# Two attention changes in one kernel: stationary values with a transposed output, and score banks shared with the transposes

## The chip, the cores and the metric

The kernel runs on one core of a Trainium2 chip. The metric is the device time of one execution in microseconds (us). TensorE is PE (its weight loads are PEld), VectorE is DVE, ScalarE is ACT, GpSimd is POOL, and SyncE (SP) issues the DMAs.

## The reference, cut to what matters

A two-layer decoder trunk on 256 tokens with model width 1024. Layer A has differential attention (6 head pairs of 2 x 64), layer B plain causal attention (12 heads of 64; with one block of 256 keys the block selection selects nothing more). Each layer also attends with 4 heads to a memory of 256 rows, and has a squared-ReLU MLP of width 4096.

```python
# memory attention, both layers: 4 heads of 64, 256 keys
p = softmax(einsum('bshd,bmhd->bhsm', qm, mk) * 64 ** -0.5);  o = einsum('bhsm,bmhd->bshd', p, mv)
# layer B: the same with a causal mask, 12 heads of 64
# layer A: w = softmax(s0) - lam * softmax(s1);  o = rmsnorm(w @ v)
x = x + concat([o_self, o_mem]) @ w_out
x = x + relu(rmsnorm(x) @ w_up) ** 2 @ w_down
```

All is float32 at the borders.

## The kernel before, in words

Every projection splits its weights and its activations into a rounded part and a rest (`wh`/`wl` for weights, `h`/`l` for activations) and sums three products. `chunk` (L308) loads one of 192 weight chunks of 128 x 1024, ACT casts it to `wh` (L328), DVE subtracts to `wl` (L330). In a mixer `nat_block` (L475) projects all 256 tokens on 512 columns, `rope` (L493 to L510) or `evac_to` (L485) takes the result out of the two `acc` banks, attention follows, and `out_proj` (L737) accumulates pair by pair in four `acc` banks. The MLPs are L785 and L787 (`wide`) and, for the last product, L846.

Attention works on two heads at a time (a "pair"; m0 and m1 are the two memory pairs, 0 to 5 the others). The steps of a pair:

- `scores` (L514): four transposes of q and k into a `t` bank (L525), a copy, the score matmuls (L555) with the 64 rows of head 0 in the upper half of the array and those of head 1 in the lower half. In layer A a causal pair first adds the mask by PE (L548); in layer B DVE adds it (`hide`, L562). Both heads lie in one buffer `s` of two PSUM banks, of which there is one. One DVE reduction for both heads (L565), the scaling of the maxima (L567, L569), then four ACT exponentials (L573); they accumulate the row sums only in layer A's causal pairs.
- `plain_T` (L614), for the memory pairs of both layers and for layer B's six pairs, so ten in all: three or four transposes of each head's probabilities (L593) into a `t` bank, then a copy (L626 or L627).
- `plain_out` (L632): the transposed probabilities are the stationary operand and the values the moving one. A 65th column of ones in the values gives the row sum. Per pair 6 (causal) or 8 (memory) matmuls with 65 columns (L644); then DVE takes a reciprocal (L652) and multiplies (L653) into `o`.
- `finish_o` (L598): two transposes of `o` (L603) into another `t` bank, then the split into `h` (ACT, L608) and `l` (DVE, L609).
- Layer A's six pairs go through `diff_T` and `diff_out` instead (transposes also L593, values L691 to L693), and then through `finish_o` with a gain.

PSUM has 8 banks: four `acc`, two `t`, and the one two-bank buffer `s`.

The order of the instructions on every engine is set when the program is built. `Plan` collects the steps with an assumed duration each, and a list scheduler sends each engine the ready step with the lowest number; a table `EARLY` shifts the numbers by kind of step and layer. A step also needs its buffers free: `acc`, `w`, `wh`, `wl` are taken first come first served. On the chip each engine then works in that order and waits on semaphores.

Of the kernel before, what the change touches and what calls it, by code (L numbers as in the profile page):

```python
# [29 lines left out]
KINDS = ("w", "mem", "nat", "stat", "rope", "score", "pt", "pv", "fin", "evac", "prep")  # L30
# [191 lines left out]
def tile_hybrid(ctx: ExitStack, tc: tile.TileContext, xt, memt, wall, gains, fgain, subln, lam, trig, out):  # L222
# [6 lines left out]
    caps = {"w": 4, "wh": 6, "wl": 6, "acc": 4, "s": 1, "t": 2, "u": 2, "sq": 2, "sqa": 2, "dg": 2,  # L229
# [38 lines left out]
    mv = fixed([128, 2, 4, 65], "mv")  # L268
    vb = fixed([128, 2, 12, 65], "vb")
# [4 lines left out]
    wu = psum.tile([128, 2, 512], F32, name="wu", tag="s0", bufs=1)  # L274
    for _ in range(34):
        nc.tensor.matmul(wu[:, 0, 0:128], ones_b, ones_b, start=True, stop=True)
# [12 lines left out]
    for t in (mv, vb):  # L289
        nc.gpsimd.memset(t[:, :, :, 64:65], 1.0)  # L290

# [222 lines left out]
    def scores(srcs, skeys, causal, sums):  # L514
# [11 lines left out]
        P.add(("pe", 4 * 85, turn), skeys, [ps])  # L526
# [10 lines left out]
        nm = fixed([128, 2, ns], "nm")  # L537
# [3 lines left out]
        sp = buf("s", [128, 2, 512], F32, psum)  # L541
# [3 lines left out]
        def qkmm():  # L545
            for hd in range(2 * pm):
                for i in range(2):
                    nc.tensor.matmul(sp.t[:, hd, i * 256:i * 256 + 128], ident_b, mask_b, start=i == 0, stop=False,  # L548
                                     skip_group_check=True)
            for qb in range(2):  # L550
                c = slice(0, n0) if qb == 0 else slice(n0, n0 + 256)
                for i, (a, b) in enumerate(passes):
                    for hd in range(2):
                        r = slice(hd * 64, hd * 64 + 64)
                        nc.tensor.matmul(sp.t[:, hd, c], qk[a].t[r, qb * 128:(qb + 1) * 128],  # L555
# [4 lines left out]
        def hide():  # L560
            o = sp.t[:, :, 0:512].rearrange("p h (b n) -> p h b n", b=4)[:, :, 0:3:2]
            nc.vector.tensor_tensor(o, o, mask_b[:, None, None, :].to_broadcast([128, 2, 2, 128]), op=OP.add)  # L562

        def mxx():
            nc.vector.tensor_reduce(nm, sp.t[:, :, 0:width].rearrange("p h (s n) -> p h s n", s=ns), axis=AX.X,  # L565
                                    op=OP.max)
            nc.vector.tensor_scalar_mul(nm, nm, -0.125)  # L567
            if causal:
                nc.vector.tensor_tensor(nm[:, :, 1], nm[:, :, 1], nm[:, :, 2], op=OP.min)  # L569

        def ex(hd, qb):
            c = slice(0, n0) if qb == 0 else slice(n0, n0 + 256)
            nc.scalar.activation(p[hd].t[:, c], sp.t[:, hd, c], AF.Exp, scale=0.125, bias=nm[:, hd, qb:qb + 1],  # L573
                                 **({"accum_out": ss[:, hd, qb:qb + 1]} if sums else {}))
        cols = 2 * 384 if causal else 2 * 512
        P.add(("pe", (4 if whole else 3) * (cols / 2.4 + 50) + 240 * pm, qkmm), qk, [sp])
        if causal and not pm:
            P.add(("dve", t_dve(512), hide), [sp], [sp])
        P.add(("dve", t_dve(2 * width) + 400, mxx), [sp], [("nm", id(nm))])
        for qb in range(2):  # L580
            for hd in range(2):
                n = n0 if qb == 0 else 256
                P.add(("act", 144 + 93 * sums + 0.835 * n, lambda hd=hd, qb=qb: ex(hd, qb)),
                      [sp, ("nm", id(nm))], [(p[hd], qb), ("ss", id(ss), 2 * hd + qb)])
        if sums:
            P.add(("dve", 90, lambda: nc.vector.reciprocal(rs, ss)), [("ss", id(ss), i) for i in range(4)],
# [583 lines left out]
```

## Time and profile before

| | us |
|---|---|
| median of 3 runs | 623.08 (623.02 to 623.41) |
| the profiled execution: its own time | 624.98 |
| its span (first to last instruction) | 623.2 |
| PE busy | 606.8 (97%) |
| DVE, ACT, POOL busy | 447.0, 373.3, 68.2 |

The median is 1.90 below the time of the profiled execution. By time in the profile: the start to 13 us, layer A's mixer to 137 us, layer A's MLP to 315 us, layer B's mixer to 437 us, layer B's MLP and the last norm to the end.

How to read it: an engine's busy time is the union of its instructions. Matmuls overlap, so the cost of a matmul in a row of them is the distance from its start to the next start, not its own length. A float32 matmul shows as two records, a transpose and an fp32r matmul as one.

### The profile page before, as it was taken

Reading aid. Unit: us, or ns where it says so; the run is one execution under the profiler, and the core shown is the slowest. Engines: PE = TensorE matmul, PEld = TensorE weight load, DVE = VectorE, ACT = ScalarE, POOL = GpSimd, SP = SyncE. Lnnn points to the kernel's source line nnn. Section 1 sums busy time; section 2 is a strip of 40 time slices with the busy share of each in tenths; the row PEclk is TensorE's granted clock in tenths of the full one; section 3 lists DMA queues with packets and bytes.
Section 4 is the critical chain, followed back from the end, with each engine's and each line's share of the span. In section 5 each row is a group of like instructions: output and inputs, shape, how many; then the busy total and the mean of one; then the engine's idle time right before and its main releaser. Section 6 shows DMA issues by size and latency. Waiting matters only on the chain.

```text
span 623.2 us, 9883 instructions
## 1 busy us (share of the span) xinstructions
PE 606.8 (97%) x3706; PEld 529.5 (85%) x3706; DVE 447.0 (72%) x764; ACT 373.3 (60%) x712; POOL 68.2 (11%) x80
## 2 busy tenths in 40 slices
PE   7988999999999999999999999999999999999995
PEld 5766778998888888888889989999888888888874
DVE  5998886778978866556785676786998788544434
ACT  6856876867766754444764655555776766433422
POOL 1532011212000000101000111310300000000002
PEclk8998999999999999999999999999999999999998
DMA  7835442345756555555566243433456556656601
GB/s 250 309 135 169 141 163 103 111 153 151 252 183 199 178 197 201 181 191 192 181 225 211 83 158 107 164 136 121 151 194 208 179 196 193 193 192 197 200 7 68
DMA packets 30865, 106.32 MB, mean 171 GB/s; under 512 B 3681, under 2 KB 4193, under 8 KB 30817
## 3 DMA queue, kind: packets, MB, share of 16 engines
q1 hardware_dynamic: 30816, 105.69, 51.7%
q8 instruction: 29, 0.48, 0.3%
q14 instruction: 20, 0.16, 0.1%
HBM read 104.62 MB, written 1.05 MB: 170 GB/s over the span
## 4 chain that ended last, share of the span: by engine, by line
PE 90%; DVE 3%; ACT 3%; DMA 2%; issue 1%; SPq 1%; POOL 0%; ACTq 0%; DVEq 0%; POOLq 0%
PE acc L785 29%; PE acc L475 17%; PE acc L787 14%; PE acc L737 7%; PE s L846 7%; PE t L846 7%; PE t L644 2%; PE s L555 2%; PE t L593 1%; DVE wl L330 1%; DMA xT<-xt 1%; PE t L525 1%; DMA w<-wall 1%; ACT B L573 1%; ACT wh L328 1%
## 5 line engine op out<-in xcount | busy, mean ns | idle before, releaser
L330 DVE TENSOR_TENSOR wl<-w,wh 128x512 fp32r<-128x512 f32 (+1 forms) x256 | 246.0, 978 | 92.0 <-ACT wh L328 88.7
L328 ACT CAST wh<-w 128x512 fp32r<-128x512 f32 (+1 forms) x256 | 208.2, 837 | 132.1 <-PE t L846 41.5
L785 PE MATMUL acc<-xn,wh 128*128 128x512 f32 x512 | 178.8, 395 | 0.0
L787 PE MATMUL acc<-xn,wl 128*128 128x256 f32 x512 | 142.4, 278 | 0.0
L785 PEld LDWEIGHTS acc<-xn,wh 128*128 128x128 f32 x512 | 96.2, 188 | 22.1
L475 PE MATMUL acc<-wh,xn 128*128 128x512 f32 (+1 forms) x320 | 96.1, 368 | 3.0 <-ACT xn L344 2.9
L787 PEld LDWEIGHTS acc<-xn,wl 128*128 128x128 f32 x512 | 96.3, 188 | 0.0
L785 PE MATMUL acc<-B,wh 128*128 128x512 f32 x256 | 88.8, 394 | 0.0
L787 PE MATMUL acc<-B,wl 128*128 128x256 f32 x256 | 71.1, 278 | 0.0
L475 PEld LDWEIGHTS acc<-wh,xn 128*128 128x128 f32 x320 | 58.2, 194 | 13.3 <-ACT xn L344 3.5
L785 PEld LDWEIGHTS acc<-B,wh 128*128 128x128 f32 x256 | 48.0, 188 | 11.2
L475 PE MATMUL acc<-wl,xn 128*128 128x512 f32 (+1 forms) x160 | 57.2, 358 | 0.0
L428 POOL TENSOR_TENSOR sqa<-sqa,sq 128x256 f32<-128x256 f32 x35 | 30.3, 866 | 231.3 <-ACT sq L427 230.0
L737 PE MATMUL acc<-B,wh 128*128 128x256 f32 x256 | 51.6, 290 | 0.0
L787 PEld LDWEIGHTS acc<-B,wl 128*128 128x128 f32 x256 | 48.1, 188 | 0.0
L758 ACT COPY u<-acc 128x256 f32<-128x256 f32 x64 | 23.5, 370 | 37.9 <-PE acc L787 37.6
L737 PEld LDWEIGHTS acc<-B,wh 128*128 128x128 f32 x256 | 41.6, 191 | 0.0
L846 PE MATMUL s<-wh,B 128*128 128x512 f32 x128 | 39.6, 391 | 0.8 <-DVE qh L878 0.8
L502 POOL TENSOR_TENSOR ropet<-ropes,trig 128x256 f32<-128x256 f32 x24 | 26.3, 1113 | 126.5 <-ACT ropes L493 92.0
L846 PE MATMUL t<-wh,B 128*128 128x512 f32 (+1 forms) x128 | 37.9, 379 | 0.0
L737 PE MATMUL acc<-B,wl 128*128 128x256 f32 x128 | 36.2, 283 | 0.0
L760 DVE TENSOR_TENSOR u<-u,acc 128x256 f32<-128x256 f32 x64 | 26.4, 417 | 12.8 <-ACT u L758 12.7
(183 smaller groups left out, 848.3 us busy)
## 6 DMA issues: line engine op xcount, KB each, us to landing
w<-wall SPq DMA_DIRECT2D x188, 512.0 KB, 4.2
w<-wall SPq DMA_DIRECT2D x8, 256.0 KB, 7.1
B<-memt SPq DMA_DIRECT2D x2, 512.0 KB, 7.2
w<-memt SPq DMA_DIRECT2D x2, 512.0 KB, 3.7
xT<-xt SPq DMA_DIRECT2D x1, 512.0 KB, 8.1
out<-qh SPq DMA_DIRECT2D x2, 256.0 KB, 2.8
out<-ql SPq DMA_DIRECT2D x2, 256.0 KB, 2.2
xT<-xt SPq DMA_DIRECT2D x2, 128.0 KB, 3.3
```

Source lines behind the costliest of these rows:

```text
L328: P.add(("act", t_act(n), lambda sl=sl: nc.scalar.copy(h.t[:, sl], w.t[:, sl])), [(w, x) for x in q], [(h, x) for x in q])
L330: P.add(("dve", t_dve(n), lambda sl=sl: nc.vector.tensor_sub(l.t[:, sl], w.t[:, sl], h.t[:, sl].bitcast(F32))), [(w, x) for x in q] + [(h, ...
L428: P.add(("pool", t_pool(S), lambda: nc.gpsimd.tensor_tensor(self.acc.t, self.acc.t, sq.t, op=OP.add)), [sq, self.acc], [self.acc])
L475: nc.tensor.matmul(pss[hf].t[:, c0:c1], a(k)[:, ts], b.t[:, o + c0:o + c1], start=(k == 0 and i == 0), stop=(k == KT - 1 and i == 2))
L502: nc.gpsimd.tensor_tensor(t.t[:, :, o:o + 32], zs.t[:, :, 32 - o:64 - o], b(sin[:, o:o + 32]), op=OP.mult)
L555: nc.tensor.matmul(sp.t[:, hd, c], qk[a].t[r, qb * 128:(qb + 1) * 128], qk[b].t[r, S:S + c.stop - c.start], start=(qb == 0 and i == 0 and ...
L737: nc.tensor.matmul(o, a.t[:, ws], x(k), start=(n == 0 and m % 2 == 0 and i == 0), stop=(n == KT - 1 and i == 2), skip_group_check=True)
L758: P.add(("act", t_act(S, True), lambda u=u, mi=mi, ps=ps: nc.scalar.copy(u.t[:, mi], ps.t[:, S:])), [ps], [(u, mi)])
L760: P.add(("dve", t_dve(S), lambda u=u, mi=mi, ps=ps: nc.vector.tensor_add(u.t[:, mi], u.t[:, mi], ps.t[:, :S])), [ps, (u, mi)], [(u, mi)])
L785: nc.tensor.matmul(ps.t, wh.t[:, ws], x_.rearrange("p a s -> p (a s)"), start=start, stop=stop, skip_group_check=True)
L787: nc.tensor.matmul(ps.t[:, 0:S], wl.t[:, ws], x_[:, 0], start=False, stop=stop, skip_group_check=True)
L846: nc.tensor.matmul(ps.t[:, c0:c1], a, b.t[:, c * 512 + c0:c * 512 + c1], start=(k == k0 and i == 0), stop=(k == 31 and i == 2), skip_group ...
```

## The change

- `plain_out`: the values (128 keys x 64 columns) become the stationary operand and the transposed probabilities the moving one, 256 columns at a time (128 for the second key block of a causal pair). Head 0 writes partitions 0 to 63 of the bank and head 1 partitions 64 to 127, so the output is already transposed. The column of ones, the reciprocal and the multiplication go; so does `finish_o` for these ten pairs. ACT and DVE split straight from the bank (L649, L650 of the changed kernel).
- `plain_T`: the probabilities are scaled by the reciprocal row sum before they are turned, by a new step `norm`: four per pair, each on DVE or on ACT as the scheduler finds (L620, L621). The row sums now come from the exponentials in all pairs.
- `scores`: the two-bank buffer `s` goes; each head gets a bank of the class `t`, which now has four. The mask of layer B, the maxima and their scaling run once per head.
- `mlp_last` takes its four banks from `t`.
- The assumed durations of several PE steps and the whole table `EARLY` are replaced, so that the order on every engine changes from start to end.

```diff
-EARLY.update(wA=70, wB=-117, memA=52, memB=-51, natA=8, natB=-63, statA=100, statB=11, ropeA=-76, ropeB=80, scoreA=89,
-             scoreB=-39, ptA=71, ptB=19, pvA=-30, pvB=158, finA=163, finB=-9, evacA=41, evacB=129, prepA=63, prepB=90)
+EARLY.update(wA=40, wB=60, memA=148, memB=-117, natA=82, natB=-5, statA=-94, statB=-135, ropeA=-84, ropeB=120,
+             scoreA=-74, scoreB=-42, ptA=95, ptB=19, pvA=-40, pvB=163, finA=201, finB=-81, evacA=-113, evacB=66,
+             prepA=25, prepB=98, normA=95, normB=-89)
...
-    caps = {"w": 4, "wh": 6, "wl": 6, "acc": 4, "s": 1, "t": 2, "u": 2, "sq": 2, "sqa": 2, "dg": 2,
+    caps = {"w": 4, "wh": 6, "wl": 6, "acc": 4, "t": 4, "u": 2, "sq": 2, "sqa": 2, "dg": 2,
...
-        sp = buf("s", [128, 2, 512], F32, psum)
+        sp = [bank("t") for _ in range(2)]
...
-        def mxx():
-            nc.vector.tensor_reduce(nm, sp.t[:, :, 0:width].rearrange("p h (s n) -> p h s n", s=ns), axis=AX.X,
-                                    op=OP.max)
-            nc.vector.tensor_scalar_mul(nm, nm, -0.125)
+        def mxx(hd):
+            m = nm[hd]
+            nc.vector.tensor_reduce(m, sp[hd].t[:, 0:width].rearrange("p (s n) -> p s n", s=ns), axis=AX.X, op=OP.max)
+            nc.vector.tensor_scalar_mul(m, m, -0.125)
...
+        cut = 128 if causal else 256
+        @early("norm")
+        def norm(hd, qb):
+            c = slice(0, cut) if qb == 0 else slice(cut, cut + 256)
+            m = c.stop - c.start
+            x, r = p[hd], (lambda: rs[:, hd, qb:qb + 1])
+            P.add([("dve", 130 + 0.52 * m, lambda: nc.vector.tensor_scalar_mul(x.t[:, c], x.t[:, c], r())),
+                   ("act", t_act(m, False, True), lambda: nc.scalar.activation(x.t[:, c], x.t[:, c], AF.Copy, scale=r()))],
+                  [(x, qb), ("rs", id(rs))], [(x, qb)], port=True)
...
         def pv():
-            first = True
-            for qb in range(2):
+            for kb in range(2):
+                q0 = 128 if causal and kb else 0
                 for hd in range(2):
-                    c = (2 * qb + hd) * 65
-                    for j, kb in blocks[qb]:
-                        nc.tensor.matmul(ps.t[:, c:c + 65], pp[hd].t[:, j * 128:(j + 1) * 128], v(kb, hd), start=first,
-                                         stop=(j, kb) == blocks[qb][-1], skip_group_check=True)
...
+                    nc.tensor.matmul(ps.t[hd * 64:hd * 64 + 64, q0:S], v(kb, hd), pp[hd].t[:, kb * S:kb * S + S - q0],
+                                     start=kb == 0, stop=kb == 1, skip_group_check=True)
...
-        def scale():
-            c = ps.t[:, 0:260].rearrange("p (a e) -> p a e", a=4)
-            nc.vector.reciprocal(ri, c[:, :, 64])
-            nc.vector.tensor_tensor(o.t.rearrange("p a (b e) -> p (a b) e", b=2), c[:, :, 0:64],
-                                    ri[:, :, None].to_broadcast([128, 4, 64]), op=OP.mult)
-        P.add(("dve", t_dve(S) + 200, scale), [ps], [o])
-        finish_o(o, kt, T)
+        P.add(("act", t_act(S, True), lambda: nc.scalar.copy(T.h(kt), ps.t[:, 0:S])), [ps], [T.hk(kt)])
+        P.add(("dve", t_dve(S), lambda: nc.vector.tensor_sub(T.l(kt), ps.t[:, 0:S], T.h(kt).bitcast(F32))),
+              [ps, T.hk(kt)], [T.lk(kt)])
```

Three places in the order. **The first** is PE in layer B's mixer, at the values of the memory pair m0 (`t<-mv` is that product, `acc` a projection, `B` a ring buffer of attention). Before:

```order
L475 MATMUL acc_3636<-wh_3525,xn_67 128x256
L644 MATMUL t_3775<-mv_78,B_685_3753 128x65 x8
L475 MATMUL acc_3642<-wh_3525,xn_67 128x256
...
L555 MATMUL s_3795<-qh_3773 128x256 x2
...
L603 MATMUL t_3813<-ident_123,o_3793 128x128 x2
```

With the change:

```order
L589 MATMUL t_3786<-ident_123,B_692_3748 128x128 x4
L473 MATMUL acc_3666<-wh_3544,xn_67 128x256
L473 MATMUL acc_3666<-wl_3565,xn_67 128x256
...
L589 MATMUL t_3798<-ident_123,B_692_3748 128x128 x4
...
L646 MATMUL t_3820<-B_696_3796,mv_78 64x256 x4
L473 MATMUL acc_3666<-wh_3605,xn_67 128x256
```

Eight matmuls of 65 columns and the two transposes of `o` became four of 256 columns on 64 output rows, and the turns of the two heads now stand apart.

**The second** is PE at layer A's first two causal pairs (4 and 5), at the mask and score matmuls. Before, with both pairs in the one buffer `s`:

```order
L548 MATMUL s_660<-mask_b_127,ident_b_125 128x128
L555 MATMUL s_660<-qh_650 128x128 x2
L555 MATMUL s_660<-qh_650 128x256 x2
L475 MATMUL acc_682<-wh_600,xn_67 128x512
...
L548 MATMUL s_732<-mask_b_127,ident_b_125 128x128
L555 MATMUL s_732<-qh_657 128x128 x2
L555 MATMUL s_732<-qh_657 128x256 x2
```

With the change:

```order
L553 MATMUL t_633<-qh_625 128x128
L553 MATMUL t_636<-qh_625 128x128
L553 MATMUL t_633<-qh_625 128x256
L553 MATMUL t_636<-qh_625 128x256
L523 MATMUL t_650<-ident_123,B_180_544 128x128 x4
...
L553 MATMUL t_675<-qh_665 128x128
L553 MATMUL t_678<-qh_665 128x128
L553 MATMUL t_675<-qh_665 128x256
L553 MATMUL t_678<-qh_665 128x256
```

The second pair has banks of its own (`t_675`, `t_678`) and stands 6 projection matmuls behind the first, where 24 stood before.

**The third** is DVE late in layer A's mixer, from the maxima of m1 to its scaling. Before:

```order
L565 TENSOR_REDUCE nm_155<-s_1026 128x4
L567 TENSOR_SCALAR nm_155<-nm_155 128x4
L330 TENSOR_TENSOR wl_1083<-w_943,wh_1069 128x512 x2
L652 RECIPROCAL ri_160<-t_1072 128x4
L653 TENSOR_TENSOR o_1097<-t_1072,ri_160 128x256
```

With the change:

```order
L564 TENSOR_REDUCE nm_158<-t_1172 128x2
L565 TENSOR_SCALAR nm_158<-nm_158 128x2
L629 COPY ppx_73<-t_1197 128x512
L564 TENSOR_REDUCE nm_159<-t_1174 128x2
L565 TENSOR_SCALAR nm_159<-nm_159 128x2
L328 TENSOR_TENSOR wl_1230<-w_1054,wh_1085 128x512 x2
L328 TENSOR_TENSOR wl_1242<-w_1120,wh_1182 128x512
L582 RECIPROCAL rs_161<-ss_160 128x4
L328 TENSOR_TENSOR wl_1242<-w_1120,wh_1182 128x512
L620 TENSOR_SCALAR B_205_673<-B_205_673,rs_161 128x256 x2
```

Before, the turn of m1 needed only the maxima and the exponentials; now the reciprocal, a weight split that stands ahead of it and the scaling come between. On PE, 24 matmuls of `out_proj`, the turns and values of m0 and the scores of pair 2 stand between the scores of m1 and its first turn.

Elsewhere in layer A, PE's first matmul for the norm's statistics (L436, L434 of the changed kernel) stands behind 87 projection matmuls instead of 45, with 9 more before the memory block's instead of 51.

## Rows read from the trace of the kernel before

**Rows 1.** The page: busy time of the engines.

```profile
PE 606.8 (97%) x3706; PEld 529.5 (85%) x3706; DVE 447.0 (72%) x764; ACT 373.3 (60%) x712; POOL 68.2 (11%) x80
```

**Rows 2.** Busy time by stage (stretch, its length, PE, PEld, DVE, ACT, POOL, then granted PE clock, DMA share, GB/s): layer A's mixer in its first two parts, layer A's MLP, layer B's mixer, layer B's MLP up to its last matmuls.

```profile
13.00:55.00 42.00, 40.00 (x181) 30.70 (x180) 39.00 (x77) 28.96 (x64) 17.07 (x18) 0.99 0.65 223
55.00:100.00 45.00, 42.62 (x253) 33.61 (x252) 36.94 (x85) 32.68 (x94) 6.44 (x8) 0.96 0.42 140
...
137.00:315.00 178.00, 178.00 (x1028) 155.57 (x1027) 133.12 (x188) 107.72 (x170) 10.89 (x11) 1.00 0.59 190
315.00:437.00 122.00, 122.00 (x977) 115.51 (x976) 85.72 (x161) 70.21 (x145) 15.02 (x14) 1.00 0.46 151
437.00:602.00 165.00, 165.00 (x861) 141.16 (x859) 112.53 (x146) 93.83 (x137) 5.17 (x7) 1.00 0.55 179
```

**Rows 3.** Waits of the whole run, those of PE in layer A's mixer and ACT's for weights: what waited, for what, us in total, times, longest us.

```profile
PE s L548 <- ACT B L573: 1.7, 1, 1.7
PE acc L475 <- ACT ropes L493: 1.5, 2, 0.9
...
PE t L603 <- DVE o L653: 0.7, 1, 0.7
...
ACT wh L328 <- DMA w<-wall: 5.4, 5, 3.4
```

**Rows 4.** PE in order of time in layer A (start, length, line, operation, tiles; in brackets the idle time before and what ended it): the wait for the buffer `s`, and two of the projection matmuls behind it.

```profile
57.21 0.38 PE L548 MATMUL s<-mask_b,ident_b 128*128 128x128 bf16 x4 [1.68 <-ACT B L573]
...
59.40 1.06 PE L475 MATMUL acc<-wh,xn 128*128 128x512 f32 x2
60.25 0.63 PE L475 MATMUL acc<-wl,xn 128*128 128x512 f32 x1
```

**Rows 5.** The granted clock just behind that wait (columns as in rows 2).

```profile
58.30:61.70 3.40, 3.40 (x10) 2.65 (x9) 3.26 (x8) 1.50 (x3) 0.93 (x2) 0.52 0.45 154
```

**Rows 6.** PE in order of time in layer B: the values of a memory pair, of a causal pair, and the transposes of an `o`, each with the projection matmuls around it.

```profile
347.24 0.28 PE L475 MATMUL acc<-wh,xn 128*128 128x256 f32 x1
347.35 1.89 PE L644 MATMUL t<-mv,B 128*128 128x65 f32 x16
349.06 0.36 PE L475 MATMUL acc<-wh,xn 128*128 128x256 f32 x1
349.26 0.28 PE L475 MATMUL acc<-wl,xn 128*128 128x256 f32 x1
...
361.85 0.38 PE L603 MATMUL t<-ident,o 128*128 128x128 f32 x2
361.99 0.48 PE L475 MATMUL acc<-wh,xn 128*128 128x512 f32 x1
362.30 0.39 PE L475 MATMUL acc<-wl,xn 128*128 128x512 f32 x1
362.53 0.39 PE L475 MATMUL acc<-wh,xn 128*128 128x512 f32 x1
...
380.35 1.45 PE L644 MATMUL t<-vb,B 128*128 128x65 f32 x12
381.61 0.37 PE L475 MATMUL acc<-wh,xn 128*128 128x256 f32 x1
```

**Rows 7.** PE in order of time in layer A: float32 score matmuls of a causal pair, the three values matmuls of a layer A pair (L691 to L693, two records each, the first shown) and the next projection, and the score matmuls of a memory pair.

```profile
48.92 0.93 PE L555 MATMUL s<-qh 64*128 64x128 f32 x8
49.78 0.51 PE L475 MATMUL acc<-wh,xn 128*128 128x512 f32 x1
...
76.68 0.38 PE L691 MATMUL t<-B,B 128*128 128x128 f32 x2
...
77.26 0.48 PE L475 MATMUL acc<-wh,xn 128*128 128x512 f32 x1
...
77.81 0.40 PE L475 MATMUL acc<-wh,xn 128*128 128x512 f32 x1
78.14 1.14 PE L555 MATMUL s<-qh 64*128 64x256 f32 x8
79.20 0.55 PE L593 MATMUL t<-ident,B 128*128 128x128 f32 x3
```

**Rows 8.** Groups of instructions by line and shape (count, busy us, mean ns of one, idle before): weight splits, maxima, accumulator reads, the scaling into `o`, the split of the output, the reciprocal, a small DVE scaling.

```profile
L330 DVE TENSOR_TENSOR wl<-w,wh 128x512 fp32r<-128x512 f32 x128 | 88.2, 723 | 16.5 <-ACT wh L328 15.6
...
L565 DVE TENSOR_REDUCE nm<-s 128x6 f32<-128x768 f32 x12 | 11.4, 951 | 0.1
L573 ACT ACTIVATION_READ_ACCUMULATOR B<-s,nm 128x1 f32 x24 | 4.9, 206 | 0.0
L653 DVE TENSOR_TENSOR o<-t,ri 128x256 f32<-128x256 f32 x10 | 4.3, 425 | 0.6
L609 DVE TENSOR_TENSOR B<-t,B 128x256 fp32r<-128x256 f32 x10 | 4.2, 420 | 3.3 <-ACT B L608 3.3
L608 ACT CAST B<-t 128x256 fp32r<-128x256 f32 x10 | 3.7, 371 | 3.4 <-PE t L603 3.1
L652 DVE RECIPROCAL ri<-t 128x4 f32<-128x4 f32 x10 | 1.8, 178 | 6.3 <-PE t L644 6.2
L453 DVE TENSOR_SCALAR dg<-ident,rstd 128x128 f32<-128x128 f32 x4 | 1.0, 282 | 0.0
```

More of the change, by code (lines that the diff above doesn't have):

```diff
@@ L513, in scores @@
     @early("score")
-    def scores(srcs, skeys, causal, sums):
+    def scores(srcs, skeys, causal):
         ps = bank("t")
@@ L525, in turn @@
                 nc.tensor.transpose(ps.t[:, i * 128:(i + 1) * 128], s(), ident)
-        P.add(("pe", 4 * 85, turn), skeys, [ps])
+        P.add(("pe", 4 * 110 + 85, turn), skeys, [ps])
         if whole:
@@ L536, in scores @@
         ns = 3 if causal else 2
-        nm = fixed([128, 2, ns], "nm")
+        nm = [fixed([128, ns], "nm") for _ in range(2)]
         ss, rs = [fixed([128, 2, 2], n) for n in ("ss", "rs")]
@@ L585, in scores @@
-        if sums:
-            P.add(("dve", 90, lambda: nc.vector.reciprocal(rs, ss)), [("ss", id(ss), i) for i in range(4)],
-                  [("rs", id(rs))])
+            nc.scalar.activation(p[hd].t[:, c], sp[hd].t[:, c], AF.Exp, scale=0.125, bias=nm[hd][:, qb:qb + 1],
+                                 accum_out=ss[:, hd, qb:qb + 1])
+        P.add(("pe", (1 if whole else 0.75) * width * 4 / 2.4 + 300 + 240 * pm, qkmm), qk, sp)
+        for hd in range(2):
+            if causal and not pm:
+                P.add(("dve", t_dve(S), lambda hd=hd: hide(hd)), [sp[hd]], [sp[hd]])
+            P.add(("dve", t_dve(width) + (420 if causal else 210), lambda hd=hd: mxx(hd)), [sp[hd]], [("nm", id(nm[hd]))])
+            for qb in range(2):
+                n = n0 if qb == 0 else 256
+                P.add(("act", 237 + 0.835 * n, lambda hd=hd, qb=qb: ex(hd, qb)),
+                      [sp[hd], ("nm", id(nm[hd]))], [(p[hd], qb), ("ss", id(ss), 2 * hd + qb)])
@@ L588, in scores @@
+        P.add(("dve", 90, lambda: nc.vector.reciprocal(rs, ss)), [("ss", id(ss), i) for i in range(4)],
+              [("rs", id(rs))])
         return p, rs
@@ L603, in turn, with plain_T @@
                 nc.tensor.transpose(ps.t[:, qb * 128:(qb + 1) * 128], o.t[:, qb], ident)
-        P.add(("pe", 170, turn), [o], [ps])
-        if gain is not None:
-            split_scaled(lambda: ps.t[:, 0:S], [ps], gain, T, kt, True)
-            return
-        P.add(("act", t_act(S, True), lambda: nc.scalar.copy(T.h(kt), ps.t[:, 0:S])), [ps], [T.hk(kt)])
-        P.add(("dve", t_dve(S), lambda: nc.vector.tensor_sub(T.l(kt), ps.t[:, 0:S], T.h(kt).bitcast(F32))),
-              [ps, T.hk(kt)], [T.lk(kt)])
-    @early("pt")
-    def plain_T(p, causal):
+        P.add(("pe", 305, turn), [o], [ps])
+        split_scaled(lambda: ps.t[:, 0:S], [ps], gain, T, kt, True)
+    def plain_T(p, rs, causal):
         n = 3 if causal else 4
```

92 lines of the change are left out of this document (35 added, 57 removed).

## The prediction

> **What bounds the kernel now.** I read the page first: PE is busy 97% of the span [rows 1]. The table by stage says where the rest is: PE is idle 2.0 us between 13 and 55 us and 2.4 us between 55 and 100 us, that is, in layer A's mixer alone; in layer A's MLP, in layer B's mixer and in layer B's MLP it is busy for all of 178, 122 and 165 us [rows 2]. DVE has 39 of 42 us taken in layer A's first part, but 86 of 122 in layer B's mixer [rows 2]. So a microsecond that PE needs less in layer B's mixer should come off the time, and in layer A's mixer it does so only where PE is not waiting. The waits are few: PE waited once for the score buffer `s` (1.7), twice for an `acc` bank that the rope still held (1.5 together), once for an `o` (0.7) [rows 3]. Behind the wait for `s` the granted clock was 0.52 for 3.4 us, the lower of its two levels, after PE had stood idle 1.68 us [rows 4, 5]; two projection matmuls took 0.85 us there, 0.43 each [rows 4], where they start 0.23 apart at the full clock [rows 6].
>
> **The sum, part by part.** It is made against the profiled execution (624.98, span 623.2) and taken from the median of 623.08, which is 1.90 lower.
>
> *Transposes of `o` gone.* The two transposes hold PE for 0.14 us, and the second projection behind them starts 0.31 later instead of 0.23, so 0.22 in all [rows 6]. Ten pairs lose them: 2.2 us. PE is the bound there, so all of it counts.
>
> *Values as the stationary operand.* Before, a memory pair holds PE for 1.71 us and a causal pair for 1.26, and either delays what follows by another 0.08 (0.20 from start to start instead of 0.12) [rows 6]: 1.79 and 1.34. The new form, two heads in two column halves, is not in this trace. The nearest rows are layer A's float32 scores, with the same columns and the two heads in two row halves. Eight records of 256 columns take 1.06 us there, four of 128 with four of 256 take 0.86 [rows 7]. The start is 0.33 behind the last projection instead of 0.23, so 0.10 is lost ahead [rows 7], and I leave 0.08 behind. The new prices are 1.24 and 1.04, and the gain is 4 x 0.55 + 6 x 0.30 = 4.0 us.
> The bounds come from the price of one record. A float32 record of 128 columns on the whole array takes 0.097 us (six in 0.58) [rows 7], one of 256 some 0.19. If the halves ran one after the other, a memory pair would cost 8 x 0.19 + 0.18 = 1.7 and a causal pair 4 x 0.29 + 0.18 = 1.3, a gain of 0.2 us over the ten. If they overlapped wholly and nothing were lost at the ends, 0.8 and 0.6: a gain of 8.6. I take 4.0, since the row halves are the same trade and carry these losses.
> A rule of the Trainium skill speaks against it. The row first: on layer B's projections each matmul has a weight load of its own (977 and 976 [rows 2]), all on the same rows of the array, and they start 0.12 apart, so the load hides behind the matmul before it [rows 6]. The Trainium skill ("TensorE: Matmul & The Clock Gate", Part 3) says that a weight load overlaps matmuls in flight only when the row groups differ, which two column halves don't offer. By that rule this term would be 0.2 us and not 4.0; the trace agrees with it for the row halves and not for the full-width loads just named.
>
> *Work put on DVE and ACT.* Ten pairs get four scalings each. DVE's nearest rows are 0.28 for 128 columns and 0.43 for a product of 256 [rows 8], so 11 to 17 us over both engines; 0.18 + 0.43 per pair goes, 6 us [rows 8]. Forty exponentials now also read the accumulator, 0.21 each, 8 us on ACT [rows 8]. The maxima run once per head, with 0.5 us more per pair. In layer B, where 34 us of DVE and 52 of ACT are free under PE [rows 2], I cost this at nothing; if that cover went, it would cost what the third rival says. In layer A only two pairs are scaled. POOL's work and the DMAs stay what they were, and the issue order of the first DMAs is unchanged; POOL sums the memory's squares later.
>
> *Waits that go.* With a bank per head, the scores of pair 5 need no exponentials of pair 4 to be done. That takes away the 1.7 and eight matmuls at 0.20 too much each, 1.6 [rows 4, 5]. The wait for `o` (0.7) [rows 3] has no `o` left to wait for. Sum: 4.0.
>
> *Waits that come.* The statistics matmul of layer A now stands 42 projections later and has 9 ahead of the memory block instead of 51, so that the memory block waits longer for the first rope: between 0 and two more of the longest such wait; I take one, 0.9 [rows 3]. In layer A's last part the path from a pair's scores to its turn now runs through a reciprocal and scalings. For m1 DVE does two maxima (0.5 + 0.17 each), a copy and three weight splits (0.72 each [rows 8]), a reciprocal and two scalings: some 5.3 us. PE has 24 matmuls of `out_proj` at 0.12, eight transposes, the values of m0 and the scores of pair 2: 2.9 + 0.9 + 1.2 + 1.2 = 6.2 us (0.12 from [rows 6], the others from above and [rows 7]). It fits with 0.9 to spare; I put in one wait of the size of the longest, 1.7 [rows 3], as an allowance over the four pairs there, between 0 and four of them. At layer B's end 12 projections (1.4 us [rows 6]) cover the last split (0.37 and 0.42 [rows 8] and the hand-overs): 0 to 0.8, I take 0.4. Sum: 3.0.
>
> The total is -2.2 - 4.0 - 4.0 + 3.0 = **-7.2 us**: 617.8 for a profiled execution, **615.9** for the median. A measurement of this kernel can tell 0.2% from no change, 1.25 us.
>
> **The rivals.**
>
> *The halves run one after the other.* For it: no row shows column halves at work. Against it: full-width weight loads hide [rows 6], and the row halves overlap [rows 7]. The values then give 0.2: -3.4 us, 619.7. The rule of the Trainium skill named above would make it so.
>
> *The wait for `s` was a wait for weights.* ACT's casts waited 5.4 us for weights, 3.4 at the longest [rows 3], and the exponentials that PE waited for stood behind such a cast. If the weights are as late now, PE waits for the cast instead and the 3.3 us of the wait and its slow stretch stay: -3.9 us, 619.2. For it: that DMA's cause, the release of weight buffers by a DVE with 39 of 42 us taken [rows 2], isn't touched.
>
> *Layer A's last part waits for the scalings* (the slower one). At m0, m1 and pairs 2 and 3 the turns stand close behind their scores on PE, on a DVE that does the weight splits of `out_proj` in between. It decides once the path of a pair grows by more than the 0.9 to spare, one weight split and a hand-over. Then each of the four places waits 1.7, and the clock falls behind three of them, 1.6 each: 11.6 instead of my 1.7, so -7.2 + 9.9 = +2.7 us, 625.8. Against it: between 55 and 100 us DVE has 8 of 45 us free and ACT 12 [rows 2], and the scalings are short.
>
> *Layer A's waits all go.* PE's idle 4.4 us and the slow stretch (1.6) vanish [rows 2, 5] and nothing comes back: -2.2 - 4.0 - 6.0 = -12.2 us, 610.9.
>
> **How the numbers follow.** My forecast gets 0.45; weights as late as before 0.22; halves one after the other 0.14; all waits gone 0.10; scalings late 0.09. The range is 611.5 to 622.0: it takes in the forecast with both ends of its waits, the two weaker gains, and most of the case in which all waits go; it leaves out the slower case, the tails of the weaker gains above 622 and the best part of the last one. Faster by over 0.2% (below 621.8) hold the forecast, the best case and most of the two weaker gains: 0.81. Within 0.2% lie weaker gains that meet more waits than I allow: 0.08. Slower gets the rest: 0.11.
>
> **What would show it.** In layer B's mixer PE should still be busy throughout, and the stage should be shorter by 8 x 0.22 + 2 x 0.55 + 6 x 0.30 = 4.7 us. A memory pair's values should hold PE for about 1.06 us and a causal pair's for 0.86 (1.5 and 1.2 if the halves take turns). PE's wait for exponentials and the stretch at half clock near 58 us should be gone; if ACT's weight cast is awaited there instead, the second rival holds. Waits of PE's transposes for DVE or ACT between 85 and 110 us would be the third. The MLPs should keep their lengths. A layer B stage that shrinks by less than 3 us, or any wait of PE in it over 1 us, would make the prediction wrong at its core.

## The result and the profile after

The changed kernel takes **618.41 us** (four runs, 617.45 to 618.53) against 623.25 for the kernel before (four runs, 623.02 to 623.68). The ratio is 0.9918, with an interval of 0.9901 to 0.9935: 4.8 us less, where 7.2 were forecast. The direction was right and the time is inside the range. The profiled execution is the one of 617.45, span 615.7.

The page first: PE has 76 matmul records less than in [rows 1], as the change says (32 in the memory pairs' values, 24 in the causal pairs', 20 in the transposes of `o`). DVE and ACT have more to do, and POOL's time is the same.

```profile
PE 601.4 (98%) x3630; PEld 519.3 (84%) x3630; DVE 453.0 (74%) x816; ACT 387.7 (63%) x780; POOL 68.2 (11%) x78
```

By stage, with the columns of [rows 2]: layer A's first part, its second part, a few microseconds of the first part, and 150 us of layer A's MLP.

```profile
13.00:55.00 42.00, 38.66 (x179) 30.04 (x179) 38.45 (x75) 30.94 (x73) 15.19 (x18) 0.96 0.63 216
55.00:100.00 45.00, 45.00 (x265) 36.29 (x265) 40.85 (x104) 35.12 (x99) 8.88 (x8) 1.00 0.41 141
...
35.10:38.40 3.30, 3.30 (x9) 2.57 (x8) 3.30 (x3) 1.39 (x4) 3.22 (x4) 0.50 0.49 159
150.00:300.00 150.00, 150.00 (x851) 130.22 (x850) 105.13 (x132) 84.73 (x123) 5.07 (x5) 1.00 0.57 193
```

PE no longer idles between 55 and 100 us, where it stood for 2.4 in the first profile of before. Between 13 and 55 it idles 3.3 us instead of 2.0. PE's waits, but for one at the very start, are these (what waited, for what, us in total, times, longest):

```profile
PE acc L473 <- ACT ropes L491: 2.7, 1, 2.7
PE acc L473 <- ACT xn L342: 2.1, 3, 1.2
...
PE acc L473 <- DVE xn L344: 1.0, 2, 0.6
```

The waits for exponentials and for an `o` of [rows 3] are gone, and no wait for a scaling has come. One wait grew: the memory block's first matmul stands until the rope has copied the bank that it needs. PE in order of time there:

```profile
31.61 0.40 PE L473 MATMUL acc<-wh,xn 128*128 128x512 f32 x1
34.72 0.51 PE L473 MATMUL acc<-wh,wh 128*128 128x512 f32 x1 [2.71 <-ACT ropes L491]
...
36.31 0.63 PE L473 MATMUL acc<-wl,wh 128*128 128x512 f32 x1
36.73 0.63 PE L473 MATMUL acc<-wh,wl 128*128 128x512 f32 x1
```

Behind a stand of 2.7 us the granted clock is 0.50, the lower level, for 3.3 us, and matmuls start 0.42 apart instead of 0.23 [rows 6].

The new values in order of time, a memory pair of layer B and a causal pair, to be laid beside [rows 6]:

```profile
345.45 0.28 PE L473 MATMUL acc<-wh,xn 128*128 128x256 f32 x1
345.66 1.08 PE L646 MATMUL t<-B,mv 128*64 128x256 f32 x8
346.68 0.38 PE L473 MATMUL acc<-wh,xn 128*128 128x256 f32 x1
346.90 0.28 PE L473 MATMUL acc<-wl,xn 128*128 128x256 f32 x1
...
370.63 0.28 PE L473 MATMUL acc<-wh,B 128*128 128x256 f32 x1
370.84 0.87 PE L646 MATMUL t<-B,vb 128*64 128x256 f32 x8
371.64 0.39 PE L473 MATMUL acc<-wh,B 128*128 128x256 f32 x1
371.87 0.28 PE L473 MATMUL acc<-wl,B 128*128 128x256 f32 x1
```

From start to start a memory pair holds PE 1.02 us (1.71 before) and a causal one 0.80 (1.26 before). The section on the prediction prices them with their ends.

What DVE and ACT got, against [rows 8] (count, busy us, mean ns): the scalings of 256 columns on both, and those of 128 on ACT.

```profile
L621 ACT ACTIVATE B<-B,rs 128x256 f32<-128x256 f32 x16 | 7.9, 524 | 0.0
...
L620 DVE TENSOR_SCALAR B<-B,rs 128x256 f32<-128x256 f32 x12 | 3.8, 348 | 0.1
...
L621 ACT ACTIVATE B<-B,rs 128x128 f32<-128x128 f32 x9 | 3.7, 410 | 0.6 <-DVE rs L582 0.6
```

**Where the time went.** The first profile of before was an execution of 624.98; a second one (below, 622.73, span 621.0) lies at its median, so the stages are compared with that. The first matmul of layer A's MLP, of layer B's mixer, of its MLP, of its last product, and the last matmul of all, in the second profile of before:

```profile
132.45 0.40 PE L785 MATMUL acc<-xn,wh 128*128 128x512 f32 x1
...
311.10 0.40 PE L475 MATMUL acc<-wh,wh 128*128 128x512 f32 x1
...
433.67 0.40 PE L785 MATMUL acc<-xn,wh 128*128 128x512 f32 x1
...
525.20 0.39 PE L846 MATMUL s<-wh,B 128*128 128x512 f32 x1
...
613.54 0.28 PE L846 MATMUL acc<-wl,B 128*128 128x256 f32 x1
```

and in the changed kernel:

```profile
129.09 0.40 PE L780 MATMUL acc<-xn,wh 128*128 128x512 f32 x1
...
310.85 0.40 PE L473 MATMUL acc<-wh,wh 128*128 128x512 f32 x1
...
427.56 0.40 PE L780 MATMUL acc<-xn,wh 128*128 128x512 f32 x1
...
520.83 0.39 PE L830 MATMUL t<-wh,B 128*128 128x512 f32 x1
...
608.01 0.28 PE L830 MATMUL acc<-wl,B 128*128 128x256 f32 x1
```

| stage | before, us | after, us | difference | forecast |
|---|---|---|---|---|
| layer A's mixer | 132.45 | 129.09 | -3.4 | -2.9 |
| layer A's MLP | 178.65 | 181.76 | **+3.1** | 0 |
| layer B's mixer | 122.57 | 116.71 | -5.9 | -4.3 |
| layer B's MLP, first product | 91.53 | 93.27 | **+1.7** | 0 |
| layer B's MLP, last product | 88.34 | 87.18 | -1.2 | 0 |
| the end | 7.4 | 7.7 | +0.2 | 0 |

Layer B's mixer gave 1.6 us more than forecast, and the MLPs, which the change doesn't touch, took 4.8 us back. PE is busy all through the MLP stages that grew, in either profile, at the full clock; it does 851 matmuls in 150 us where it did 867.

Layer A's mixer can't be read as finely. It took 134.68 us in the first profile of before and 132.45 in the second, while every later stage repeats within 0.02 us between the two. Part of its -3.4 lies ahead of all attention; the stretch from 13 to 16 us (columns of [rows 2]), in the second profile of before and in the changed kernel:

```profile
13.00:16.00 3.00, 3.00 (x9) 2.31 (x9) 3.00 (x5) 2.87 (x7) 1.18 (x2) 0.56 0.83 277
```

```profile
13.00:16.00 3.00, 2.37 (x10) 1.62 (x10) 2.95 (x5) 3.00 (x8) 0.25 (x1) 1.00 0.80 260
```

The granted clock was 0.56 there before and 1.00 with the change. The experiments follow two questions: what each part is worth, and why the MLPs are longer.

### The profile page after: what moved, and what is told of

Read it like the earlier page. It is cut to its first block, busy times and chain, and to the rows that moved or that the text cites. A ratio compares the mean times of both kernels' runs of the same rounds, so it can differ in the third digit from the quotient of the medians.

```text
span 615.7 us, 9865 instructions
## 1 busy us (share of the span) xinstructions
PE 601.4 (98%) x3630; PEld 519.3 (84%) x3630; DVE 453.0 (74%) x816; ACT 387.7 (63%) x780; POOL 68.2 (11%) x78
## 4 chain that ended last, share of the span: by engine, by line
PE 93%; DMA 3%; DVE 1%; ACT 1%; issue 1%; SPq 0%; ACTq 0%; DVEq 0%
PE acc L780 29%; PE acc L473 19%; PE acc L782 15%; PE t L830 14%; PE acc L732 8%; PE t L553 2%; DMA w<-wall 2%; PE t L589 2%; PE t L646 1%; PE t L523 1%; DMA xT<-xt 1%; ACT wh L326 0%; SPq L303 0%; PE acc L830 0%; DVE wl L328 0%
## 5 line engine op out<-in xcount | busy, mean ns | idle before, releaser
L780 PE MATMUL acc<-xn,wh 128*128 128x512 f32 x512 | 181.8, 398 | 0.0
L473 PE MATMUL acc<-wh,xn 128*128 128x512 f32 (+1 forms) x320 | 90.3, 357 | 3.0 <-ACT xn L342 2.1
L780 PE MATMUL acc<-B,wh 128*128 128x512 f32 x256 | 90.5, 399 | 0.0
L830 PE MATMUL t<-wh,B 128*128 128x512 f32 (+1 forms) x256 | 77.4, 384 | 0.0
L782 PE MATMUL acc<-B,wl 128*128 128x256 f32 x256 | 71.9, 281 | 0.0
L473 PEld LDWEIGHTS acc<-wh,xn 128*128 128x128 f32 x320 | 56.0, 188 | 14.2 <-ACT xn L342 3.1
L830 PEld LDWEIGHTS t<-wh,B 128*128 128x128 f32 x256 | 47.7, 188 | 9.6
L473 PE MATMUL acc<-wl,xn 128*128 128x512 f32 (+1 forms) x160 | 55.4, 346 | 0.0
L830 PE MATMUL t<-wl,B 128*128 128x512 f32 (+1 forms) x128 | 49.2, 384 | 0.0
```

The costliest lines, as they stand in the source:

```text
L473: nc.tensor.matmul(pss[hf].t[:, c0:c1], a(k)[:, ts], b.t[:, o + c0:o + c1], start=(k == 0 and i == 0), stop=(k == KT - 1 and i == 2))
L780: nc.tensor.matmul(ps.t, wh.t[:, ws], x_.rearrange("p a s -> p (a s)"), start=start, stop=stop, skip_group_check=True)
L782: nc.tensor.matmul(ps.t[:, 0:S], wl.t[:, ws], x_[:, 0], start=False, stop=stop, skip_group_check=True)
L830: nc.tensor.matmul(ps.t[:, c0:c1], a, b.t[:, c * 512 + c0:c * 512 + c1], start=(k == k0 and i == 0), stop=(k == 31 and i == 2), skip_group ...
```

## The experiments

Ratios are to the kernel before, run in the same session; medians of the kernel before there were 622.4 to 622.9.

### The parts one at a time

The values alone: the kernel before with `plain_out`, `plain_T` and `turned` of the change, one double score bank and the old table. One buffer is 64 bytes longer than in the change, as in the next run.

```
-    mv = fixed([128, 2, 4, 65], "mv")
+    mv = fixed([128, 2, 4, 64], "mv")
-        return plain_T(prs[0], True)
+        return plain_T(*prs, True)
...
     sp = buf("s", [128, 2, 512], F32, psum)
```

> The kernel before with the values stationary, the output transposed and the probabilities scaled first, but with the old double score bank and the old table of priorities; tiles on the old grid. My forecast priced this part at -2.2 (no transposes of o), -4.0 (shorter holds) and -0.7 (no wait for o): about 616.5 us if all of it is on the path. Rival: the new scalings delay the exps and the turns while there is only one score bank, so that half of it comes back as waits on exps or scalings: about 620 us.

Measured: **618.36 us** (617.75 to 619.69), ratio 0.9938 (0.9926 to 0.9951). Between theory and rival: 4.1 us less. Against the second profile of before, layer B's mixer fell by 5.2 us, layer A's by 2.6, and the MLPs grew by 3.5 in this program as well. PE waits neither for exponentials nor for scalings in this profile, so nothing came back as a wait. Two of its waits of PE, one at the start, one at the end:

```profile
PE acc L472 <- ACT xn L341: 2.9, 2, 2.1
...
PE s L842 <- DVE qh L874: 0.8, 1, 0.8
```

A later run of the same code with that buffer at another length (last in the next section) does wait for exponentials, less than the kernel before in either profile (1.7 and 0.7):

```profile
PE s L545 <- ACT B L570: 0.5, 1, 0.5
```

The values and the pooled banks: the changed kernel with the old table.

```
-EARLY.update(wA=40, wB=60, memA=148, ... normA=95, normB=-89)
+EARLY.update(wA=70, wB=-117, memA=52, ... prepA=63, prepB=90)
```

> The changed kernel with the old table of priorities, tiles on the old grid: the part above and the pooled banks, one score bank per head, but not the new order. My forecast priced the pooled banks at -1.7 (the wait for exps) and -1.6 (the stretch at half clock after it), so about 3.3 us under the kernel with the values alone, and 613 us if the table does nothing. Rival: with four banks in one pool and the old priorities the scores take the banks that the turns need, and it is no faster than the values alone.

Measured: **615.72 us** (615.16 to 616.14), ratio 0.9891 (0.9877 to 0.9904), so the pooled banks give 2.6 us; the rival falls. But they give most of it elsewhere than I said: between the two profiles 1.5 in layer A's mixer, 0.8 in layer B's and 1.2 in the last product. The last two repeat in two further runs at other places (layer B's mixer 117.38 against 116.58, the last product 88.37 against 87.18); the 1.5 is within what layer A's mixer differs between two executions of one kernel. The 1.2 comes with the wait for `qh` shown above: two quarters of the last product lay in the two halves of the one double buffer, and a matmul into it waited until DVE had added the other quarter to `qh`. This program, with a bank for each, has no such wait. It is also 2.0 us **faster than the change with its new table** (617.72, next section, with its tiles at the same place): the new order of priorities costs more than it gives. At another place (next section) the old table is 1.4 us ahead, 617.16 against 618.55, with intervals that overlap. Of all that ran, this is the fastest version.

### The longer MLPs

In every MLP pair a matmul of 512 columns is followed by one of 256. In the profile of before the two took 346 ns together (867 matmuls in 150 us), in the changed kernel 353 (851); from the 65th pair of each product on the spacing is even. The change moves all later buffers, since `mv` and `vb` are narrower. So the change was given 64 bytes back, the kernel before was shifted by 64 bytes, and the kernel before was profiled again.

```
-    vb = fixed([128, 2, 12, 64], "vb")
+    vb = fixed([128, 1552], "vb")[:, 0:1536].rearrange("p (a b c) -> p a b c", a=2, b=12)
```

> The changed kernel with one allocation made 64 bytes longer, so that the weight and hidden-layer tiles stand where they stood against a 128-byte grid before the change; no instruction is added or moved. Place theory: the wide pairs of the two MLPs took 353 ns in the changed kernel and 346 ns before because those tiles moved by 64 bytes; here the pairs are back at 346 ns, MLP A is 3 us shorter (181.8 to 178.7), the up part of MLP B 1.7 us shorter, and the median about 613.7 us. Rival (the order of casts and copies, or the PSUM banks, slow the pairs): nothing changes, 353 ns and 618.4 us.

```
-    ones_b = fixed([128, 128], "ones_b", BF)
+    ones_b = fixed([128, 160], "ones_b", BF)[:, 0:128]
```

> The kernel before with one allocation made 64 bytes longer, so that the same tiles stand 64 bytes off; nothing else. Place theory: the pairs go from 346 to 353 ns, 768 of them, and the median from 623.2 to about 628. Rival (order or banks): no change, 623.2 us.

> The kernel before once more, unchanged, for a second profile of it. In its first profile the wide pairs of the MLPs took 346 ns; in the five other kernels so far they took 351 to 353 ns. If that is a property of the program (where its tiles stand), this profile shows 346 ns again, MLP A at 178.7 us and MLP B's up part at 91.5 us. Rival (it was a matter of that one execution): 351 to 353 ns, MLP A about 181.5 us and B's up part 92.8 us; then the two first profiles can't be compared stage by stage there.

Measured: the padded change 617.72 (616.39 to 618.67), ratio 0.9925 (0.9911 to 0.9938), no different from the change, with the pairs at 351 ns in the first products and 353 in layer A's second. The shifted kernel before: **626.29** (625.47 to 627.12), ratio 1.0062 (1.0049 to 1.0074): 3.8 us **slower**, by 64 bytes of place alone. In its profile layer A's MLP is 3.1 us longer than in the second profile of before and the first product of layer B's 1.5, while layer B's mixer is 0.7 shorter (121.89). The second profile of before: 622.73. Windows of the same lengths in the two MLPs (columns of [rows 2]): the kernel before, again,

```profile
150.00:300.00 150.00, 150.00 (x867) 131.16 (x866) 107.89 (x136) 87.36 (x129) 5.08 (x5) 1.00 0.58 197
460.00:515.00 55.00, 55.00 (x319) 48.10 (x318) 45.15 (x61) 38.01 (x61) 0.00 (x0) 1.00 0.55 191
```

and the kernel before shifted by 64 bytes:

```profile
150.00:300.00 150.00, 150.00 (x851) 130.15 (x850) 106.58 (x132) 86.58 (x125) 5.06 (x5) 1.00 0.58 194
460.00:515.00 55.00, 55.00 (x313) 47.73 (x312) 45.03 (x62) 37.73 (x61) 0.00 (x0) 1.00 0.54 190
```

867 against 851 matmuls in the same 150 us, and 319 against 313 in the same 55, PE busy throughout and the clock full in both. The groups by line and shape between 140 and 225 us say that the matmuls take 3 to 4 ns more each, while DVE's weight splits keep their length (1237 and 1238 ns) and the weight loads theirs (188 ns). Before, again:

```profile
L785 PE MATMUL acc<-xn,wh 128*128 128x512 f32 x235 | 81.9, 395 | 0.0
L787 PE MATMUL acc<-xn,wl 128*128 128x256 f32 x236 | 65.5, 277 | 0.0
```

Shifted:

```profile
L785 PE MATMUL acc<-xn,wh 128*128 128x512 f32 x236 | 83.7, 398 | 0.0
L787 PE MATMUL acc<-xn,wl 128*128 128x256 f32 x237 | 66.6, 281 | 0.0
```

So the kernel before has the short spacing in both of its profiles, and 64 bytes destroy it. That left the question which place brings it back. Three more programs were put at chosen places: the change with its weight tiles 128 bytes past a 1024-byte grid, as in the kernel before; the change with the old table, likewise; and, in the next section, the change with four old numbers, with `wh` and `wl` as before within 2048 bytes.

```
-    vb = fixed([128, 2, 12, 64], "vb")
+    vb = fixed([128, 1776], "vb")[:, 0:1536].rearrange("p (a b c) -> p a b c", a=2, b=12)
```

> The changed kernel with one allocation made 960 bytes longer, so that the weight tiles stand at the same place within 1024 bytes as before the change (128 past the grid, like the tile xn that they multiply); no instruction is added or moved. 64 bytes alone gave 351 instead of 353 ns. Place theory, within 1024 bytes: pairs at 346 ns, MLP A 3 us and MLP B's up part 1.7 us shorter, about 613.7 us. Rival (place plays no part beyond the 64 bytes): 351 ns as with 64 bytes, about 617.7 us.

> The changed kernel with the old table of priorities (615.7 us with its tiles 256 bytes past the 1024-byte grid), now with its weight tiles 128 past it as before the change. Place theory: pairs at 346 ns and about 611 us, the shortest so far. Rival: 351 ns and 615.7 us.

Measured: 618.55 (615.17 to 620.57), ratio 0.9932 (0.9907 to 0.9957), and 617.16 (616.64 to 617.41), ratio 0.9908 (0.9888 to 0.9928). Both miss; the pairs stay at 353 ns. The 1024-byte form of the place theory falls, and so does its 2048-byte form in the run further below.

The last try was the sharpest: the values alone on the kernel before, with every weight buffer and `xn` at exactly the addresses of before, the same banks and the same table. Its edit is shown against the run of the values alone.

```
-    vb = fixed([128, 1552], "vb")[:, 0:1536].rearrange("p (a b c) -> p a b c", a=2, b=12)
+    vb = fixed([128, 1648], "vb")[:, 0:1536].rearrange("p (a b c) -> p a b c", a=2, b=12)
```

> The kernel before with the values stationary (the run of that part alone, 618.4 us), with one allocation made 384 bytes longer, so that every buffer of weights (w, wh, wl), xn, ropes, ropet and qh, and the hidden-layer tiles but B3, stand at exactly the addresses that they have in the kernel before; the PSUM banks and the table are also those of before. So far padding the changed kernel by 64, 960 and 1984 bytes left the wide pairs at 351 to 353 ns, and moving the kernel before by 64 bytes took it from 346 to 353. Theory (places on the chip alone decide, but those of the whole set): pairs at 346 ns, MLP A at 178.7 us, and the time 4 to 4.7 us under the run without the padding: about 614 us. Rival (something else that the new program carries decides, and 64 bytes merely tipped it): 351 to 353 ns and 618.4 us; then what sets the pairs' spacing stays open.

Measured: 618.70 (617.47 to 618.99), ratio 0.9930 (0.9908 to 0.9952), no gain over the values alone. But its two windows differ:

```profile
150.00:300.00 150.00, 150.00 (x851) 130.05 (x850) 105.27 (x134) 85.32 (x126) 5.06 (x5) 1.00 0.56 193
460.00:515.00 55.00, 55.00 (x319) 48.48 (x318) 44.95 (x62) 37.54 (x61) 0.00 (x0) 1.00 0.56 192
```

Layer A's MLP runs at 851 in 150 us, the long spacing, and layer B's at 319 in 55, the short one, in one execution with the same weight buffers. So the addresses of the weights and of `xn` alone don't fix the spacing. Behind its first pairs a product keeps its spacing to its end; what picks it **stays open**.

### The wait for the first rope

In the changed kernel's trace the first rope copy on ACT began when a chain of root instructions on DVE had ended; a row of each, from the timelines of the two engines:

```profile
33.78 0.16 DVE L397 TENSOR_TENSOR rstd<-rstd,rst 128x2 f32<-128x2 f32 x1
```

```profile
33.98 0.69 ACT L491 ACTIVATE ropes<-acc,rstd 128x512 f32<-128x512 f32 x1
```

The chain and the matmul ahead of it were emitted earlier, by hand:

```
+    steps = [s for s in P.order() if s not in root[1:]]
+    i = steps.index(root[0]) + 1 + 40
+    for st in steps[:i] + root[1:] + steps[i:]:
-    for st in P.order():
```

> The changed kernel with two steps taken out of the planned order and put earlier: the matmul of layer A's first statistic (at 29.3 us in the changed kernel's trace) and its chain of root instructions on DVE behind it, about 4 us sooner. In the trace that chain ended at 33.9 us, the first rope copy began at 33.98, and PE stood 2.7 us, then ran eight matmuls of the memory block at 427 ns instead of 229. My theory: the late chain is the cause of both; the first rope copy starts by about 32.2, the wait falls to under 1 us and the slow stretch goes, so 2 to 3.5 us less: 615 to 616.5 us. Rival: the copy waits for something else (ACT's casts ahead of it), or the weight remainders that the chain now delays on DVE make PE wait about as long: 618 us.

Measured: **621.09 us** (619.73 to 621.81), ratio 0.9976 (0.9964 to 0.9988), 2.7 us slower than the change. Neither theory nor rival. The chain did end early, at 28.7; but the rope copy came later, at 37.37. ACT, DVE and the first of POOL's sums in order of time:

```profile
34.93 0.42 ACT L425 ACTIVATE sq<-B 128x256 f32<-128x256 f32 x1 [2.53 <-POOL sqa L426]
...
37.37 0.68 ACT L491 ACTIVATE ropes<-acc,rstd 128x512 f32<-128x512 f32 x1
```

```profile
30.62 3.69 DVE L328 TENSOR_TENSOR wl<-w,wh 128x512 fp32r<-128x512 f32 x6
```

```profile
31.14 3.76 POOL L426 TENSOR_TENSOR sqa<-sqa,sq 128x256 f32<-128x256 f32 x1 [10.29 <-ACT sq L425]
```

The new table puts the memory's squares late. They stand ahead of the rope copy in ACT's queue, with two buffers between them and POOL's sums. With the chain gone from there, six weight splits ran on DVE without a pause from 30.6 to 34.3. POOL's first sum, begun at 31.14, took 3.76 us and ended 0.6 behind the last split; the four sums after it, with DVE idle, took 0.72 each. ACT waited 2.5 us for that one sum, the rope for ACT, PE for the rope: 5.1 us. So the four early numbers of the old table were put back:

```
-EARLY.update(wA=40, ... memA=148, ... natA=82, ... statA=-94, ...
+EARLY.update(wA=70, ... memA=52, ... natA=8, ... statA=100, ...
```

> The changed kernel with four numbers of the table set back to the old ones, those that place layer A's first weights, the memory's splits and squares and the first projections (wA, memA, natA, statA). The run with the root chain moved alone was slower (621.1): the chain then ended at 28.7 us, yet the first rope copy began at 37.4, behind squares of the memory on ACT that waited up to 2.5 us for POOL's sums. My new theory: the squares, put late, stand ahead of the rope copy on ACT; put early again they are out of the way, PE waits under 1 us for the first rope, no stretch at half clock follows, and the time is 2 to 3.5 us under the changed kernel: 614.5 to 616 us. Rival: the early part gains that, but the old numbers shift later steps and give it back, 617 to 618 us.

> The kernel with the four old numbers and one allocation made 1984 bytes longer, so that the weight tiles wh and wl stand at the same place within 2048 bytes as in the kernel before and as the tile xn that they multiply (128 past it); 64 and 960 bytes did not bring the short pairs back, while moving the kernel before by 64 bytes took them away. Place theory, within 2048 bytes: pairs in the up parts of the MLPs at 346 ns, 1.4 us less in each of the two, and with the down part 4 us less in all: about 611 us. Rival (some other feature of the old places is needed): 353 ns, no gain over the kernel with the four old numbers alone.

Measured: 617.32 us (617.21 to 618.03), ratio 0.9911 (0.9889 to 0.9934), and with the other place 617.35 (615.16 to 618.13), 0.9901 (0.9873 to 0.9929). The wait for ropes fell to 1.4 and 1.6 us in all, 1.0 at the longest, as in the kernel before. The time did not follow: against the change at most 1 us, which these intervals don't separate. The rival is nearer: in the first of the two, waits of 0.7 for an `o` and 0.5 for a weight remainder came in, and layer A's mixer took 129.9 us instead of 129.1.

### The column halves

The values' matmuls were put in another order, so that neighbours write the same half:

```
-            for kb in range(2):
-                q0 = 128 if causal and kb else 0
-                for hd in range(2):
+            for hd in range(2):
+                for kb in range(2):
+                    q0 = 128 if causal and kb else 0
```

> The changed kernel with the values' matmuls in another order: both key blocks of the first head, then both of the second, so that neighbours write the same column half and not alternate ones. Theory: it is the alternation of column halves that makes two matmuls run side by side (8 records in 1.01 us); without it a memory pair holds PE for 1.5 to 1.8 us and a causal one for 1.2 to 1.4, and the time grows by 3 to 5 us, to about 622. Rival: order plays no part (each record is just short), 1.01 us and 618.4.

Measured: 617.27 us (615.98 to 618.69), ratio 0.9909 (0.9878 to 0.9940), no change. My theory of alternation falls: the records take 0.01 us more, if anything.

```profile
363.24 1.09 PE L646 MATMUL t<-B,mv 128*64 128x256 f32 x8
...
369.37 0.88 PE L646 MATMUL t<-B,vb 128*64 128x256 f32 x8
```

Eight records of 256 columns at 0.19 each would be 1.5 us one after the other, and PE is busy with them for 1.1. That could also mean that each record is short, the rival of this run. The single records decide it: in the trace they start in twos, 0.013 us apart here and 0.007 in the changed kernel, and two follows two after 0.20 to 0.27 us. The first two of this memory pair:

```profile
363.24 0.44 PE L646 MATMUL t<-B,mv 128*64 128x256 f32 x2
```

So two records run side by side in either order. That they are one of each head is likely but not shown; a run with both heads in one half wasn't made.

## Why the prediction was right, and where it was wrong

**Transposes of `o`, -2.2.** Right, though not measured by itself: they are gone, PE was busy around them, and the twenty records are among the 76. With the values alone layer B's mixer, where PE doesn't wait, fell by 5.2 us; this term and the next had 4.7 for it.

**Values stationary, -4.0.** Right, a little too small. With the start 0.09 later than behind a projection and 0.10 lost behind, a memory pair costs 1.21 us (1.24 forecast) and a causal one 1.00 (1.04): 4 x 0.58 + 6 x 0.34 = 4.4. The rival of halves that take turns falls (1.02 and 0.80, not 1.5 and 1.2). The rule that spoke against it, of the Trainium skill ("TensorE: Matmul & The Clock Gate", Part 3), that a weight load overlaps matmuls in flight only for other row groups, gave 0.2 us for this term as I read it; the rows of two column halves don't bear that reading out, in either order.

**Work on DVE and ACT, 0.** Right. ACT's scalings took 0.41 and 0.52, more than the 0.28 to 0.43 that I had for one, and DVE's 0.35 for 256 columns; all forty took some 16 us, inside the 11 to 17, and no wait of PE names them. The slower rival needed such waits between 85 and 110 us; there is none.

**Waits that go, -4.0.** The waits went, but the size came from one execution: in the second profile of before the wait for `s` is 0.7 and not 1.7, and nothing behind it is slow, so against that profile this term was worth 1.4. With the values alone the wait was gone in one run and 0.5 in another, so the pooled banks took away little of it. They gave 2.6 us, mostly by other ways, 1.2 of it in the last product, of which my list had nothing although the profile of before had the wait for `qh` (0.8). Two rows of PE's waits in the second profile of before:

```profile
PE s L846 <- DVE qh L878: 0.8, 1, 0.8
PE s L548 <- ACT B L573: 0.7, 1, 0.7
```

The rival of late weights falls: no wait of PE in layer A's middle is for a weight cast.

**Waits that come, +3.0.** Near in sum by luck; each term was mis-sized. PE's waits for ropes are 2.7 us in all, in one piece, where they were 1.5 and 1.1 in the two profiles of before, and some 1.6 of slow matmuls stand behind it (eight at 0.20 too much): about 3 us more, not 0.9; the place was right. The slow part is no fixed price: behind stands of 2.3 us (the run with the values in another order) and 2.5 (the change padded by 64 bytes) at this place the clock stayed at 1.00. I had read the matmul's place in PE's order, and not the squares that the table moved in front of the rope copy on ACT: in the changed kernel ACT's last step ahead of the copy ends at 33.87 and the root chain at 33.94, so moving the chain alone could gain little. Layer A's last part has no wait at all, not 1.7, and layer B's end none.

**The MLPs keep their lengths.** This is the step that failed: +4.8 us. I had costed the change at nothing there because no instruction of the MLPs changes. The shift of 64 bytes in the kernel before, which also changes no instruction there, shows +3.8 us by the same spacing. That the change's own shift of addresses is the cause is not shown: with the weights back at the old addresses one MLP was short and the other long. Without this loss the sum of the other stages would have been -10.2 between the two profiles, 3 more than forecast: -3.4 and -5.9 in the mixers and -1.2 in the last product. Of this, layer A's share is uncertain by some 2 us, and 0.7 of layer B's may be place as well, since the shift alone gave that much there. Two errors of opposite sign left the total within 2.5 us; that is luck.

**What stays open:** what chooses between the two spacings of an MLP, and which of the new table's other numbers cost what the old one (615.72) doesn't.

## What to carry to other kernels

Before a saving of a few microseconds is credited to a change, compare the spacing of matmuls in stretches that it does not touch: here they moved when nothing but the place of buffers had changed, by nearly as much as the change is worth. Profile the kernel before twice when a term rests on a wait that occurs once; 1.7 us of wait and 1.6 of slow clock were 0.7 and nothing in the next execution. When a step is moved on one engine, look in the queue of the engine that it waits for, too: a rope copy stood behind squares that stood behind another engine's sums. And time a re-tuned order against the old order with the same code: here the old one was 2.0 us better at one place of the buffers and 1.4 at another.

## What the runs showed of the hardware

- Wide matmul pairs ran at 346 or at 351 to 353 ns, with the full clock, equal LDWEIGHTS (188 ns) and no waits, evenly from the 65th pair of a product on. Moving the buffers by 64 bytes took the short spacing away; identical weight addresses gave the long one in one MLP and the short one in the next.
- The records of the two heads' values, in two column halves, start in twos 0.007 to 0.014 us apart, even when four records of one half are issued ahead of the other's (1.09 against 1.08 us busy).
- POOL's sum of 256 columns takes 0.72 to 0.74 us alone. Begun beside a run of six weight splits on DVE without a pause, one took 3.76 us and ended 0.6 behind the last of them. In reverse, root instructions on two columns took 0.6 us beside POOL's sums in the changed kernel: `rst<-rstd` from 30.59 to 31.23, with the sum ending at 31.21. With the chain moved ahead of those sums it took 0.16 (at 27.19).
- Stands of PE of 1.7 and 2.7 us were followed by 3.4 and 3.3 us at the lower clock (0.52 and 0.50); stands of 2.3 and 2.5 us in two other runs were not (1.00).
